# Fewer blocks by seven products, a swiglu gate by Silu, and the last pair of blocks in the down projection's stream

## The chip, the core and the metric

The kernel runs on one core of a Trainium2 chip. The core has five engines with queues of their own: TensorE (PE: matmuls and transposes; its weight loads are listed apart as PEld), VectorE (DVE), ScalarE (ACT), GpSimd (POOL) and SyncE (SP, which here only issues DMAs). Each works through its instructions in order; a semaphore lets one wait for another. The metric is the device time of one execution, in microseconds (us); lower is better.

## The reference

Input x is 256 frames of 2048 features in fp32. Two layers follow each other, each a token mixer (gated linear attention in the first, sparse attention in the second) and a swiglu; a last norm ends it. The part that matters here is the swiglu, which each layer has once:

```python
def swiglu(h, w1, w3, w2):
    return (jax.nn.silu(h @ w1) * (h @ w3)) @ w2

x = x + swiglu(rmsnorm(x, norm_ffn[i]), ffn_w1[i], ffn_w3[i], ffn_w2[i])
```

w1 and w3 are 2048 x 5632, w2 is 5632 x 2048, all fp32. silu(z) is z times the sigmoid of z, which is also z/2 (1 + tanh(z/2)).

## The kernel before

**Numbers in halves.** TensorE takes fp32r operands. To keep fp32's precision every operand is split into a high part (a rounded copy, by ScalarE) and a low part (the rest, by VectorE), and every product is three matmuls: high x high, high x low, low x high. `split_w` (L131 to 137) does this for a weight tile of 512 rows by 512 columns, 128 x 2048 in SBUF: one cast on ScalarE into `wh` (L135), one subtraction on VectorE into `wl` (L136). `wh` and `wl` have three buffers each. A raw weight tile is 1 MB; four buffers (`raw`) hold such tiles. All these loads are issued on SP's queue. `gemm` does the same by L191 and L192.

**The swiglu, `ffn` (L499 to 539).** The 5632 hidden features are cut into 11 blocks (b = 0 to 10) of 512. For a block, x (256 frames in two halves, t = 0 and 1; 2048 features in two halves of eight 128-row slices) is multiplied by 512 columns of w1 and of w3. There are two ways:

- `plain` (L449 to 474): eight products of 128 frames by 1024 features by 512 columns, two of them summed for each of four outputs. That is 8 weight tiles, 8 splits and 192 matmuls of 128 x 128 x 512 (L463). The operands of x are kept as forms: A11, A12, N22 and F7 (a difference of the two halves of frames); the second frame half is got as the first product minus or plus a correction.
- `pair` (L368 to 447): the four blocks of w1 and w3 are taken together with the four of x, as a 2 x 2 matrix product by seven products instead of eight. The operands of x are sums and differences made once per layer (forms A11, A12, N22, F3, F5, F6, F7); the operands of the weights are sums of raw tiles. Some sums are made by VectorE (`plus`, L405), some by a DMA from memory that adds into the tile (`plus_dma`, L408), which goes by GpSimd's queue. It takes 168 matmuls (L393), 8 plain loads, 4 accumulating loads of 1 MB, 14 splits and 4 sums of 128 x 2048 on VectorE. The products come in the order A11, F5, F3, F6, F7, A12, N22. The first operand pair `va` is changed in place by the accumulating loads (after F5 by w3's second half, after F6 by w1's second half), and N22 reads it last. Four tiles hold `va` and `vb`: v0 and v1, and v2 and g3; which pair holds which alternates with `turn`, b // 2 % 2 (L412 to 414). With turn 0, `va` is in v0 and v1.

Both give their results to `done` (L508 to 515): for the first of a frame half, the gate: a Tanh on ScalarE (L512) and a VectorE operation (L513); for the second, a product with it (L515). The result `u` is transposed by TensorE and split (`split_t`, L208 to 219) into one of three operand tiles `g0` to `g2`. `split_t` is a generator in the list `side`, and the matmul loops run one step of it every few matmuls (`tick`).

**The down projection, `pieces` (L476 to 497).** For two blocks that are finished, w2's 1024 rows are multiplied in eight pieces (four output column groups, two blocks), each one weight tile and 24 matmuls (L489 to 491), and the sum is added to x. `ffn` keeps these generators in `down` and runs one piece at each `yield` of the block under way; a pair has eight yields.

**Which way a block takes** is decided by `if down` (L517). After blocks 1, 3, 5 and 7 a down projection is put into `down` (L533). Its eight pieces run in blocks 2, 4, 6 and 8. The generator has then given its eight pieces but has not ended, so that it still stands in `down` when the next block begins, and is dropped at that block's first yield. So blocks 2 to 9 are pairs, the even ones with eight pieces beside them and the odd ones with none; 0, 1 and 10 are plain. The three blocks 8, 9 and 10 are left over, and `residual` multiplies them by w2 after the layer, group by group of output columns, three weight tiles and 72 matmuls for each of four groups. `residual` also adds to x and starts the next norm of each group (`update`, L263; transposes on TensorE, a scaled copy on ScalarE, its low part on VectorE). After the last layer it ends with the final norm (`gemm_tail`, `final`, `last`).

**The order.** The instructions of an engine stand in an order that a scheduler makes from the program; it may move splits, loads and transposes ahead.

Of the kernel before, what the change touches and what calls it, by code (L numbers as in the profile page):

```python
# [12 lines left out]
F32 = mybir.dt.float32  # L13
F32R = mybir.dt.float32r
BF16 = mybir.dt.bfloat16
AF = mybir.ActivationFunctionType
ALU = mybir.AluOpType
AX = mybir.AxisListType

P = 128  # L20
SEQ = 256
NT = SEQ // P
DM = 2048
NB = 512
# [31 lines left out]
def trunk(  # L56
# [7 lines left out]
    nc = tc.nc  # L64
    PS = bass.MemoryType.PSUM
    cst = ctx.enter_context(tc.tile_pool(name="cst", bufs=1))
# [3 lines left out]
    sm = ctx.enter_context(tc.tile_pool(name="sm", bufs=2))  # L70
# [13 lines left out]
            nc.sync.dma_start(x[t][n], x2[t, :, n * NB:(n + 1) * NB])  # L84


    neghalf = cst.tile([P, 8], F32, name="neghalf")
    nc.gpsimd.memset(neghalf, -0.5)
    warm = sm.tile([P, 8], F32, tag="warm", bufs=1, name="warm")
# [4 lines left out]
    cols = cst.tile([P, 72], F32, name="cols")  # L94


    sm.tile([P, 8], F32, tag="pad", bufs=1, name="pad")

    def gains(c0, srcs):

# [30 lines left out]
    def split_w(raw, pool=wp):  # L131

        wh = pool.tile([P, 4, NB], F32R, tag="wh", bufs=3 if pool is wp else 1, name="wh")
        wl = pool.tile([P, 4, NB], F32R, tag="wl", bufs=3 if pool is wp else 1, name="wl")
        nc.scalar.copy(wh, raw)  # L135
        nc.vector.tensor_sub(wl, raw, wh.bitcast(F32))  # L136
        return wh, wl
# [204 lines left out]
    def scaled(r, f, tag, w=NT):  # L342
        o = sm.tile([P, w], F32, tag=tag, name=tag)
        nc.gpsimd.tensor_scalar_mul(o, r, f)
        return o
# [17 lines left out]
    def flush():  # L363
        while side:
            tick()


    def pair(nrm, wa, wb, c0, turn, done):  # L368

        def src(w, j, c):
            r = j * 1024 + c * 512
            return w[r:r + 512, c0:c0 + NB].rearrange("(k p) n -> p k n", p=P)

        def load(w, j, homes):
            o = []
            for c, (pool, tag, bufs) in enumerate(homes):
                raw = pool.tile([P, 4, NB], F32, tag=tag, bufs=bufs, name=tag)
                nc.sync.dma_start(raw, src(w, j, c))  # L380
                o.append(raw)
            return o

        def product(acc, raws, form, start, stop, then=None):
            for c in range(2):
                wh, wl = split_w(raws[c])
                if then is not None:
                    then(c)
                hi, lo = nrm.forms[form]
                for j in range(4):  # L390
                    k = 4 * c + j
                    for i, (l_, r_) in enumerate(((hi, wh), (hi, wl), (lo, wh))):
                        nc.tensor.matmul(acc, l_[:, k, :], r_[:, j, :], start=start and k == i == 0,  # L393
                                         stop=stop and k == 7 and i == 2, skip_group_check=not start)
                    if j % 2:
                        tick()

        def bank():
            return acc_p.tile([P, NB], F32, tag="acc", name="acc")

        def sums(tag):
            return nrm.pool.tile([P, NB], F32, tag=tag, bufs=1, name=tag)

        def plus(dst, other):
            return lambda c: nc.vector.tensor_add(dst[c], dst[c], other[c])  # L405

        def plus_dma(dst, w, j):
            return lambda c: nc.gpsimd.dma_start(dst[c], src(w, j, c), accum_op=ALU.add)  # L408

        fz = nrm.pool  # L410
        stream = [(wp, "raw", RAW)] * 2
        homes = [((fz, "v0", 1), (fz, "v1", 1)), ((fz, "v2", 1), (res, "g3", 1))]  # L412
        va = load(wa, 0, homes[turn])
        vb = load(wb, 0, homes[1 - turn])
        b1 = bank()
        product(b1, va, "A11", True, True, plus(va, vb))
        s1 = sums("s1")
        nc.scalar.copy(s1, b1)
        yield
        b2 = bank()  # L420
        product(b2, va, "F5", True, True, plus_dma(va, wb, 1))
        y = sums("y")
        nc.vector.tensor_sub(y, b2, s1)
        yield
        vc = load(wb, 1, stream)
        product(b2, vc, "F3", False, True, plus(vb, vc))
        yield
        b3 = bank()
        product(b3, va, "F6", True, True, plus_dma(va, wa, 1))
        w = sums("w")  # L430
        nc.vector.tensor_sub(w, b3, s1)
        yield
        product(b3, vb, "F7", False, True)
        nc.vector.tensor_add(w, w, b2)
        nc.vector.tensor_add(y, y, b3)
        yield
        vd = load(wa, 1, stream)
        product(b1, vd, "A12", False, True)
        done("11", b1)
        done("12", w)  # L440
        yield
        product(b3, va, "N22", False, True)
        nc.vector.tensor_sub(s1, s1, b3)
        done("21", s1)
        done("22", y)
        yield
        yield

    def plain(nrm, ws, c0, done):  # L449

        for q, w in zip("12", ws):
            acc = [acc_p.tile([P, NB], F32, tag="acc", name="acc") for _ in range(3)]
            for g in range(4):
                raw = wp.tile([P, 4, NB], F32, tag="raw", bufs=RAW, name="raw")
                nc.sync.dma_start(raw, w[g * NB:(g + 1) * NB, c0:c0 + NB].rearrange("(k p) n -> p k n", p=P))
                wh, wl = split_w(raw)
                for bank, form, start, stop in ((0, "A11", True, True), (1, "F7", True, True)) if g < 2 else \
                        ((0, "A12", False, True), (2, "N22", True, True)):
                    hi, lo = nrm.forms[form]
                    for j in range(4):  # L460
                        k = 4 * (g % 2) + j
                        for i, (l_, r_) in enumerate(((hi, wh), (hi, wl), (lo, wh))):
                            nc.tensor.matmul(acc[bank], l_[:, k, :], r_[:, j, :], start=start and k == i == 0,  # L463
                                             stop=stop and k == 7 and i == 2, skip_group_check=not start)
                        if j % 2:
                            tick()
                if g == 1:
                    s1 = nrm.pool.tile([P, NB], F32, tag="s1", bufs=1, name="s1")
                    nc.scalar.copy(s1, acc[0])
                    nc.vector.tensor_add(s1, s1, acc[1])  # L470
                    yield
            nc.vector.tensor_sub(s1, s1, acc[2])
            done("1" + q, acc[0])
            done("2" + q, s1)
# [24 lines left out]
    def ffn(layer, nrm):  # L499

        w1, w3, w2 = ffn_w1[layer], ffn_w3[layer], ffn_w2[layer]
        sc = {}
        parts = []
        down = deque()
        for b in range(DFF // NB):
            us = [None] * NT

            def done(q, v):  # L508
                t = int(q[0]) - 1
                if q[1] == "1":  # L510
                    us[t] = cm.tile([P, NB], F32, tag="u", name="u")
                    nc.scalar.activation(us[t], v, AF.Tanh, scale=sc["h"][:, t:t + 1])  # L512
                    nc.vector.scalar_tensor_tensor(us[t], us[t], 1.0, v, op0=ALU.add, op1=ALU.mult)  # L513
                else:
                    nc.vector.scalar_tensor_tensor(us[t], us[t], sc["r2"][:, t:t + 1], v, op0=ALU.mult, op1=ALU.mult)  # L515

            for slot, _ in enumerate(pair(nrm, w1, w3, b * NB, b // 2 % 2, done) if down else plain(nrm, (w1, w3), b * NB, done)):  # L517
                if b == 0 and slot == 0:
                    flush()
                    r = nrm.rstd()  # L520
                    sc["h"] = scaled(r, 0.5, "rh")
                    sc["r2"] = sm.tile([P, NT], F32, tag="r2", name="r2")
                    nc.gpsimd.tensor_tensor(sc["r2"], r, sc["h"], op=ALU.mult)
                while down:
                    try:
                        next(down[0])
                        break
                    except StopIteration:
                        down.popleft()
            hi, lo = hi_lo(b % 3)  # L530
            side.append(split_t(us, hi, lo))
            parts.append((hi, lo, b * NB))
            if b % 2 and b < 8:  # L533
                down.append(pieces(w2, parts))
                parts = []
        while down:
            for _ in down.popleft():
                pass
        return w2, parts
# [480 lines left out]
    with tc.tile_pool(name="gp", bufs=2) as gp:  # L1020
        n0.begin(gp)
        down = gla(n0, gp)
        flush()
    with tc.tile_pool(name="fz0", bufs=1) as fz:
        n1.begin(fz)
        residual(gla_w_out[0], down, n1.update)
        down = ffn(0, n1)
        flush()
    with tc.tile_pool(name="dp", bufs=2) as dp:
# [3 lines left out]
        down = dsa(n2, dp)  # L1033
        flush()
    with tc.tile_pool(name="fz1", bufs=1) as fz:
        n3.begin(fz)
        residual(dsa_w_out[0], down, n3.update)
        down = ffn(1, n3)
# [57 lines left out]
```

## Time and profile before

| | us |
|---|---|
| median of 3 runs | 2426.34 (2423.76 to 2428.74) |
| the profiled execution | 2430.86 |
| its span, first to last instruction | 2429.1 |
| TensorE busy | 2281.5 (94%) |
| VectorE busy | 1645.9 (68%) |
| ScalarE busy | 1183.5 (49%) |
| GpSimd busy | 112.8 (5%) |

In the profile, a group's row has the source line, the engine, the operation, its output and inputs with their sizes, how often it ran, then busy time and the mean time of one in ns, then the idle time of the engine just before it and what ended it. A row of a timeline has start and duration in us, and in brackets how long the engine had idled and for what. A row of a stage (start:end) has its length, then busy time and count of instructions for PE, PEld, DVE, ACT and POOL, the granted clock of TensorE as a share, the busy share of the DMA engines, and GB/s. "SPq" is a DMA issue on SP's queue.

The queues of DMAs moved 493 MB in this execution; GpSimd's accumulating loads are 64 of 1 MB.

### The profile page before, as it was taken

How to read it: one execution, taken by the hardware profiler on the slowest of the kernel's cores; microseconds unless marked ns; L12 is line 12 of the kernel's file. 1: busy time of each engine (PE TensorE's matmuls, PEld its weight loads, DVE VectorE, ACT ScalarE, POOL GpSimd, SP SyncE). 2: the span in 40 equal slices, each digit the busy share in tenths (PEclk: the TensorE clock that was granted, in tenths of full speed). 3: DMA queues.
4: the chain of work that ended last, by engine and by line, in shares of the span. 5: the costliest groups of instructions: out<-in, count | busy, mean ns of one | idle time of the engine just before them, and what ended most of it. 6: DMA issues, size and time to landing. Idle time of an engine off the chain costs nothing.

```text
span 2429.1 us, 25156 instructions
## 1 busy us (share of the span) xinstructions
PE 2281.5 (94%) x10199; PEld 1857.5 (76%) x10199; DVE 1645.9 (68%) x1348; ACT 1183.5 (49%) x1053; POOL 112.8 (5%) x159
## 2 busy tenths in 40 slices
PE   9999999998897979989999999999988979889798
PEld 7888888876675867768888888888876867768687
DVE  6555456677886878865556655565786778878754
ACT  5545455454454445544444454454444545545443
POOL 0000000000000000000100000000000000000000
PEclk9999999999999989999999999999998999989899
DMA  8555466586877968775554545566677977779663
GB/s 280 164 174 180 148 219 232 172 233 194 232 242 207 286 184 222 229 205 187 182 173 139 191 157 174 174 219 212 176 235 201 293 182 225 230 190 311 138 218 112
DMA packets 254773, 493.36 MB, mean 203 GB/s; under 512 B 8200, under 2 KB 20832, under 8 KB 254528
## 3 DMA queue, kind: packets, MB, share of 16 engines
q1 hardware_dynamic: 219856, 423.33, 51.1%
q0 software_dynamic: 33792, 67.11, 16.0%
q8 instruction: 80, 1.31, 0.2%
q10 hardware_dynamic: 1008, 1.31, 0.2%
q14 instruction: 37, 0.30, 0.0%
HBM read 489.59 MB, written 2.12 MB: 202 GB/s over the span
## 4 chain that ended last, share of the span: by engine, by line
PE 59%; issue 21%; DMA 9%; DVE 8%; ACT 2%; POOL 1%; SPq 0%; POOLq 0%; ACTq 0%; DVEq 0%
PE acc L201 11%; PE acc L203 11%; PE acc L202 11%; PE acc L463 10%; DMA g<-in_ffn_w 6%; PE acc L393 6%; DVE wl L136 5%; DMA v<-in_ffn_w 3%; PE down L490 2%; ACT wh L135 2%; PE down L491 2%; PE down L489 2%; DVE v L405 1%; POOL v L408 1%; PE trq L827 0%
## 5 line engine op out<-in xcount | busy, mean ns | idle before, releaser
L192 DVE TENSOR_TENSOR wl<-raw,wh 128x2048 fp32r<-128x2048 f32 (+3 forms) x161 | 350.1, 2176 | 314.8 <-ACT wh L191 314.6
L136 DVE TENSOR_TENSOR wl<-raw,wh 128x2048 fp32r<-128x2048 f32 x179 | 409.5, 2289 | 184.7 <-ACT wh L135 184.7
L135 ACT CAST wh<-raw 128x2048 fp32r<-128x2048 f32 x179 | 342.3, 1912 | 392.6 <-PE down L491 144.3
L191 ACT CAST wh<-raw 128x2048 fp32r<-128x2048 f32 (+3 forms) x161 | 291.9, 1815 | 278.8 <-PE acc L203 217.7
L136 DVE TENSOR_TENSOR wl<-v,wh 128x2048 fp32r<-128x2048 f32 x120 | 272.7, 2286 | 83.1 <-ACT wh L135 83.1
L201 PE MATMUL acc<-wh,hh 128*128 128x512 f32 (+3 forms) x832 | 327.1, 393 | 0.0
L135 ACT CAST wh<-v 128x2048 fp32r<-128x2048 f32 x120 | 227.4, 1904 | 198.9 <-DMA v<-in_ffn_w 99.9
L203 PE MATMUL acc<-wh,hl 128*128 128x512 f32 (+3 forms) x832 | 318.4, 383 | 0.0
L202 PE MATMUL acc<-wl,hh 128*128 128x512 f32 (+3 forms) x832 | 317.0, 381 | 0.5 <-DVE wl L192 0.5
L393 PE MATMUL acc<-wh,fhF 128*128 128x512 f32 x512 | 216.5, 426 | 59.3 <-ACT wh L135 59.2
L393 PE MATMUL acc<-wl,fhF 128*128 128x512 f32 x512 | 216.0, 422 | 30.9 <-DVE wl L136 30.9
L490 PE MATMUL down<-wl,g 128*128 128x512 f32 x512 | 204.0, 398 | 9.3 <-DVE wl L136 9.3
L393 PE MATMUL acc<-wh,flF 128*128 128x512 f32 x512 | 212.2, 414 | 0.0
L491 PE MATMUL down<-wh,g 128*128 128x512 f32 x512 | 202.9, 396 | 0.0
L489 PE MATMUL down<-wh,g 128*128 128x512 f32 x512 | 200.3, 394 | 0.0
L203 PEld LDWEIGHTS acc<-wh,hl 128*128 128x128 f32 x832 | 156.2, 188 | 30.8
L202 PEld LDWEIGHTS acc<-wl,hh 128*128 128x128 f32 x832 | 156.6, 188 | 30.3 <-issue 1.7
L201 PEld LDWEIGHTS acc<-wh,hh 128*128 128x128 f32 x832 | 156.5, 188 | 28.9 <-issue 1.9
L393 PEld LDWEIGHTS acc<-wh,fhF 128*128 128x128 f32 x512 | 103.9, 205 | 91.2 <-ACT wh L135 68.3
L201 PE MATMUL acc<-wh,g 128*128 128x512 f32 x424 | 167.2, 394 | 0.0
L203 PE MATMUL acc<-wh,g 128*128 128x512 f32 x424 | 165.5, 390 | 0.0
L202 PE MATMUL acc<-wl,g 128*128 128x512 f32 x424 | 165.4, 390 | 0.0
(282 smaller groups left out, 3608.6 us busy)
## 6 DMA issues: line engine op xcount, KB each, us to landing
raw<-in_ffn_w SPq DMA_DIRECT2D x200, 1024.0 KB, 5.8
v<-in_ffn_w SPq DMA_DIRECT2D x48, 1024.0 KB, 6.6
v<-in_ffn_w POOLq DMA_DIRECT2D x48, 1024.0 KB, 9.4
raw<-in_dsa_w_in SPq DMA_DIRECT2D x48, 1024.0 KB, 5.1
raw<-in_gla_w_in SPq DMA_DIRECT2D x40, 1024.0 KB, 5.1
raw<-in_gla_w_out SPq DMA_DIRECT2D x16, 1024.0 KB, 5.2
g<-in_ffn_w SPq DMA_DIRECT2D x16, 1024.0 KB, 6.7
g<-in_ffn_w POOLq DMA_DIRECT2D x16, 1024.0 KB, 13.3
```

Source lines behind the costliest of these rows:

```text
L135: nc.scalar.copy(wh, raw)
L136: nc.vector.tensor_sub(wl, raw, wh.bitcast(F32))
L191: a = nc.scalar.copy(wh[:, sl, :n], raw[:, sl, :n])
L192: v = nc.vector.tensor_sub(wl[:, sl, :n], raw[:, sl, :n], wh[:, sl, :n].bitcast(F32))
L201: nc.tensor.matmul(acc[t][:, :n], hi[:, k, ts_], wh[:, k, :n], start=start, stop=False)
L202: nc.tensor.matmul(acc[t][:, :n], hi[:, k, ts_], wl[:, k, :n], start=False, stop=False)
L203: nc.tensor.matmul(acc[t][:, :n], lo[:, k, ts_], wh[:, k, :n], start=False, stop=last)
L393: nc.tensor.matmul(acc, l_[:, k, :], r_[:, j, :], start=start and k == i == 0, stop=stop and k == 7 and i == 2, skip_group_check=not start)
L463: nc.tensor.matmul(acc[bank], l_[:, k, :], r_[:, j, :], start=start and k == i == 0, stop=stop and k == 7 and i == 2, skip_group_check=not ...
L489: nc.tensor.matmul(acc[t], hi[:, k, ts_], wh[:, k, :], start=start, stop=False)
L490: nc.tensor.matmul(acc[t], hi[:, k, ts_], wl[:, k, :], start=False, stop=False)
L491: nc.tensor.matmul(acc[t], lo[:, k, ts_], wh[:, k, :], start=False, stop=last)
```

## The change

There are three parts.

1. A block is a pair only if b is 2, 4, 6, 8 or 10; the others (0, 1, 3, 5, 7, 9) are plain. And a down projection is put into `down` after every odd block, so also after 9. It runs in block 10. `residual` is left with one part, block 10, for each layer: 24 matmuls for each of four groups in place of 72.
2. The gate: `Silu` on ScalarE with the norm's factor r as its scale, in place of `Tanh` with r/2 and VectorE's (tanh + 1) times z. The second VectorE operation multiplies with r. Two small GpSimd operations per layer go. Silu is in another activation table than Exp and Tanh: the built program has three more table loads, one ahead of the first Silu of each layer and one ahead of the first Exp of the sparse attention.
3. Two unused tiles. One of 64 bytes at the start of the first pool, and one enlarged by 64 bytes where two tiles of 32 bytes (`r2`) are gone. All the tiles that are used thereby lie 64 bytes further, and keep their distances.

```diff
+    cst.tile([P, 16], F32, name="pad")
...
-    sm.tile([P, 8], F32, tag="pad", bufs=1, name="pad")
+    sm.tile([P, 24], F32, tag="pad", bufs=1, name="pad")
...
-                    nc.scalar.activation(us[t], v, AF.Tanh, scale=sc["h"][:, t:t + 1])
-                    nc.vector.scalar_tensor_tensor(us[t], us[t], 1.0, v, op0=ALU.add, op1=ALU.mult)
+                    nc.scalar.activation(us[t], v, AF.Silu, scale=sc["r"][:, t:t + 1])
                 else:
-                    nc.vector.scalar_tensor_tensor(us[t], us[t], sc["r2"][:, t:t + 1], v, op0=ALU.mult, op1=ALU.mult)
-
-            for slot, _ in enumerate(pair(nrm, w1, w3, b * NB, b // 2 % 2, done) if down else plain(nrm, (w1, w3), b * NB, done)):
+                    nc.vector.scalar_tensor_tensor(us[t], us[t], sc["r"][:, t:t + 1], v, op0=ALU.mult, op1=ALU.mult)
+
+            for slot, _ in enumerate(pair(nrm, w1, w3, b * NB, b // 2 % 2, done) if b in range(2, 11, 2) else plain(nrm, (w1, w3), b * NB, done)):
                 if b == 0 and slot == 0:
                     flush()
                     r = nrm.rstd()
-                    sc["h"] = scaled(r, 0.5, "rh")
-                    sc["r2"] = sm.tile([P, NT], F32, tag="r2", name="r2")
-                    nc.gpsimd.tensor_tensor(sc["r2"], r, sc["h"], op=ALU.mult)
+                    sc["r"] = r
...
-            if b % 2 and b < 8:
+            if b % 2:
                 down.append(pieces(w2, parts))
                 parts = []
```

The order moves with it. On SP's queue, where block 2 of layer 0 ends and block 3 begins, before (L482 loads the down projection's weights, L380 a pair's; the v and g tiles named are block 3's vb and va, then block 4's va):

```order
L380 DMA v_4058<-in_ffn_w 128x4x512
L380 DMA v_4060<-in_ffn_w 128x4x512
L482 DMA raw<-in_ffn_w 128x4x512 x2
L380 DMA raw<-in_ffn_w 128x4x512 x2
L380 DMA v_4054<-in_ffn_w 128x4x512
L380 DMA g_4056<-in_ffn_w 128x4x512
L380 DMA raw<-in_ffn_w 128x4x512 x2
L482 DMA raw<-in_ffn_w 128x4x512 x2
L380 DMA v_4337<-in_ffn_w 128x4x512
L380 DMA v_4339<-in_ffn_w 128x4x512
```

The same place of the changed kernel (L483 and L381 are these lines now, L456 loads a plain block's weights; v_4320 and v_4322 are block 4's va, v_4324 and g_4326 its vb):

```order
L381 DMA v_4320<-in_ffn_w 128x4x512
L381 DMA v_4322<-in_ffn_w 128x4x512
L483 DMA raw<-in_ffn_w 128x4x512 x2
L456 DMA raw<-in_ffn_w 128x4x512 x2
L381 DMA v_4324<-in_ffn_w 128x4x512
L381 DMA g_4326<-in_ffn_w 128x4x512
L456 DMA raw<-in_ffn_w 128x4x512 x6
L483 DMA raw<-in_ffn_w 128x4x512 x2
```

All of block 4's operands are now asked for while block 2 ends, between the second and the third of block 3's eight weight tiles.

On ScalarE, at the end of layer 0's swiglu, before (L469 and L470 of the kernel before belong to block 10, L191 casts the weights of the residual stage, `g` is block 10's operand, L240 is the next norm):

```order
L469 COPY s_7013<-acc 128x512
L191 CAST wh<-raw 128x2048 x3
L787 DMA kvb<-in_dsa_kv_norm 128x256
L217 CAST g_7079<-tr 128x512 x2
L789 DMA kib<-in_dsa_kidx_norm 128x128
L191 CAST wh<-raw 128x2048 x3
L240 ACTIVATE junk,ssq<-x_81 128x512
```

The same place of the changed kernel (L192 casts the residual stage's weights, L513 is the gate):

```order
L192 CAST wh<-raw 128x2048
L513 ACTIVATE u<-s_6813,rstd 128x512
L785 DMA kvb<-in_dsa_kv_norm 128x256
L192 CAST wh<-raw 128x2048
L787 DMA kib<-in_dsa_kidx_norm 128x128
L192 CAST wh<-raw 128x2048
L218 CAST g_7292<-tr 128x512 x2
L192 CAST wh<-raw 128x2048
```

Three casts of residual weights stand ahead of the two copies of block 10's operand in both; in the changed kernel the first residual matmul needs these copies, where before it needed those of block 8. With three buffers for `wh`, the third of the casts takes the one that the last piece's matmuls read.

On VectorE, the same place of the changed kernel (L193 makes the low parts of the residual weights, L497 adds the last piece to x, L219 makes the low parts of block 10's operand, L356 adds the first residual group to x):

```order
L444 TENSOR_TENSOR s_6813<-s_6813,acc 128x512
L193 TENSOR_TENSOR wl<-raw,wh 128x2048
L515 SCALAR_TENSOR_TENSOR u<-u,rstd,y 128x512
L193 TENSOR_TENSOR wl<-raw,wh 128x2048
L497 TENSOR_TENSOR x_87<-x_87,down_7228 128x512
L497 TENSOR_TENSOR x_88<-x_88,down_7229 128x512
L193 TENSOR_TENSOR wl<-raw,wh 128x2048
L219 TENSOR_TENSOR g_7292<-tr,g_7292 128x512 x2
L356 TENSOR_TENSOR x_81<-x_81,acc_7319 128x512
```

The low part of the third residual weight stands ahead of block 10's low parts. On TensorE the eight transposes of block 10 stand directly behind the last piece and ahead of the first residual matmul, and the sequence of blocks 4, 6, 8 and 10 is that of block 2, matmul for matmul.

## The prediction

> **What bounds the kernel now.** I read the page first (TensorE is busy for 94% of the span, so time is lost only where it waits), then busy time by stage over both feed-forward layers. The stages are cut at the first matmul of each block, which the timeline of TensorE shows by its line and tiles. In order: blocks 0 and 1 together; blocks 2, 3, 4, 5 and 6; blocks 2 to 9 together; block 10; the residual stage.
>
> ```profile
> PE 2281.5 (94%) x10199; PEld 1857.5 (76%) x10199; DVE 1645.9 (68%) x1348; ACT 1183.5 (49%) x1053; POOL 112.8 (5%) x159
> ```
>
> ```profile
> core 0: us, PE busy (x) PEld busy (x) DVE busy (x) ACT busy (x) POOL busy (x), PEclk, DMA share, GB/s
> 395.86:485.92 90.06, 90.03 (x402) 73.62 (x400) 56.78 (x46) 42.00 (x39) 1.87 (x3) 1.00 0.64 210
> 485.92:571.08 85.16, 83.33 (x370) 68.23 (x369) 69.50 (x46) 44.62 (x27) 5.41 (x4) 1.00 0.85 247
> 571.08:630.64 59.56, 44.48 (x177) 34.10 (x176) 40.28 (x26) 28.29 (x18) 5.17 (x4) 0.91 0.77 200
> 630.64:718.20 87.56, 84.01 (x369) 68.22 (x368) 76.45 (x50) 45.53 (x28) 5.19 (x4) 1.00 0.83 248
> 718.20:777.60 59.40, 44.69 (x177) 34.15 (x176) 40.28 (x26) 28.30 (x18) 5.19 (x4) 0.91 0.77 200
> 777.60:866.09 88.49, 84.34 (x370) 68.12 (x368) 76.39 (x50) 45.33 (x28) 5.19 (x4) 1.00 0.83 246
> 485.92:1072.00 586.08, 516.59 (x2178) 411.91 (x2177) 461.56 (x294) 294.41 (x183) 41.71 (x32) 0.96 0.80 222
> 1072.00:1117.24 45.24, 45.24 (x206) 37.11 (x204) 27.29 (x21) 19.63 (x16) 0.00 (x0) 1.00 0.61 210
> 1117.24:1186.05 68.81, 68.81 (x320) 56.68 (x318) 38.47 (x35) 31.54 (x38) 0.68 (x4) 1.00 0.54 174
> ```
>
> Blocks 0, 1 and 10 (plain) and the residual stage keep TensorE full. Block 2 (a pair beside a down projection) is nearly full. Blocks 3, 5, 7 and 9 are pairs with nothing beside them: some 59 us for 168 matmuls, with TensorE busy for 45. The chain of waits gives the full pace, 24 matmuls in 5.49 us, so 0.2288 us each:
>
> ```profile
> 669.19 5.49 PE acc L393 x24
> ```
>
> 168 such matmuls are 38.4 us. What holds an odd block is the chain of its four accumulating loads on GpSimd's queue, each issued when the one before has landed (first and last of four), behind which ScalarE's split and then the last product wait:
>
> ```profile
> 580.42 1.28 POOL L408 DMA_DIRECT2D v<-in_ffn_w  x1 [49.62 <-issue]
> ...
> 609.99 1.30 POOL L408 DMA_DIRECT2D g<-in_ffn_w  x1 [7.63 <-DVE wl L136]
> 623.71 1.91 ACT L135 CAST wh<-g 128x2048 fp32r<-128x2048 f32 x1 [4.64 <-DMA g<-in_ffn_w]
> ```
>
> From 580.4 to 623.7 is 43 us for four loads. In an even block the down projection's 192 matmuls cover the same chain.
>
> **The change, part by part.** Sums are against the profiled execution: span 2429.1 us, 2430.86 in all, 4.5 us above the median of the runs, 2426.34.
>
> *Odd blocks, pair to plain.* Each goes from 168 matmuls to 192, loses its accumulating loads, and becomes what blocks 0 and 1 are: 90.06/2 = 45.03 us with their transposes. Four cost 180.1 us.
>
> *Even blocks.* Block 2 is now the model of all five (4, 6, 8 now follow a plain block as it does; 10 becomes one), in the same order on TensorE. Its 85.16 us hold one wait of 2.25 us: the second half of the F6 product needs the second accumulating load.
>
> ```profile
> 520.44 1.91 ACT L135 CAST wh<-g 128x2048 fp32r<-128x2048 f32 x1 [6.88 <-DMA g<-in_ffn_w]
> ```
>
> In blocks whose accumulating loads go to v0 and v1 (4 and 8) the F6 product ran at full pace (the row at 669.19 is block 4's). So I take 85.16 for 2, 6, 10 and 85.16 - 2.25 = 82.9 for 4 and 8: 421.3 us in layer 0. Bounds: no such wait anywhere (-6.8), and 2.25 us in all five (+4.5).
>
> In layer 1 the rows are, in order, block 2, blocks 2 to 9, block 10, the residual stage, and what follows the last matmul:
>
> ```profile
> 1718.69:1802.95 84.26, 83.10 (x369) 68.14 (x368) 69.39 (x46) 44.63 (x27) 5.23 (x4) 1.00 0.85 249
> 1718.69:2309.38 590.69, 527.15 (x2177) 421.85 (x2176) 461.86 (x294) 294.86 (x183) 41.53 (x32) 0.93 0.79 221
> 2309.38:2354.60 45.22, 45.22 (x205) 37.11 (x204) 27.46 (x21) 19.62 (x16) 0.00 (x0) 1.00 0.61 210
> 2354.60:2421.00 66.40, 66.24 (x295) 54.30 (x293) 35.32 (x32) 26.15 (x28) 0.56 (x1) 1.00 0.42 142
> 2421.00:2429.10 8.10, 0.00 (x0) 0.00 (x0) 2.03 (x5) 2.06 (x4) 0.55 (x1) 0.79 0.35 130
> ```
>
> Its five even blocks: 3 x 84.26 + 2 x 82.9 = 418.6. Up to the residual stage, then: layer 0 goes from 586.08 + 45.24 = 631.3 to 421.3 + 180.1 = 601.4 (**-29.9**), layer 1 from 590.69 + 45.22 = 635.9 to 598.7 (**-37.2**).
>
> *Residual stage, three parts to one.* 288 matmuls become 96, 22.0 us. It now starts with block 10's own operand, which nothing covers. In the order of ScalarE and VectorE given above, the split of a third residual weight stands ahead of the copies of that operand, and this split needs the buffer that the last down matmuls read. The same wait stands behind block 2:
>
> ```profile
> 571.32 1.91 ACT L135 CAST wh<-v 128x2048 fp32r<-128x2048 f32 x1 [3.52 <-PE down L491]
> 573.13 0.58 ACT L217 CAST g<-tr 128x512 fp32r<-128x512 f32 x1
> ...
> 573.74 0.69 DVE L218 TENSOR_TENSOR g<-tr,g 128x512 fp32r<-128x512 f32 x1
> ```
>
> ```profile
> L136 DVE TENSOR_TENSOR wl<-raw,wh 128x2048 fp32r<-128x2048 f32 x179 | 409.5, 2289 | 184.7 <-ACT wh L135 184.7
> ```
>
> From the last down matmul (571.08): 0.24 to the split, 1.91, its low part on VectorE 2.29, the operand's low part 0.69, with 0.1 between: 5.2 us, in which TensorE does eight transposes and two matmuls. Entry costs 5.2 - 0.4 = 4.8 us beyond the 96 matmuls, twice; bounds 0.8 (eight transposes alone, at the 0.1 us each that comes next) and 7.1 (one more split on VectorE in front). Layer 0 keeps the transposes of the next norm: 68.81 - 288 x 0.2288 = 2.9 us for 28, so 2.5 for 24. Layer 0: 4.8 + 22.0 + 2.5 = 29.3 against 68.81 (**-39.5**). What could spill is VectorE's work per output group: the low parts of the norm's operand cost
>
> ```profile
> L256 DVE SCALAR_TENSOR_TENSOR hl<-tr,cols,hh 128x256 fp32r<-128x256 f32 x32 | 13.7, 477 | 5.5 <-ACT hh L253 5.5
> ```
>
> each, and four of them, two x updates of 0.69 and one split of 2.29 are 5.6 us beside TensorE's 5.5 + 0.6. I take no spill; with one it is about a microsecond in each of four groups.
>
> Layer 1: 4.8 + 22.0 = 26.8 to the last matmul and 8.2 behind it, against 66.40 + 8.10. The final tile of the first half used to finish 8.2 us ahead of the second; now it is 12 matmuls, 2.75 us. VectorE needs 3.7 us from one x update to the end of its last scaling:
>
> ```profile
> 2412.62 0.69 DVE L1057 TENSOR_TENSOR x<-x,acc 128x512 f32<-128x512 f32 x1 [5.96 <-PE acc L154]
> ...
> 2415.59 0.75 DVE L1064 SCALAR_TENSOR_TENSOR x<-x,rf,nf 128x512 f32<-128x512 f32 x1
> ```
>
> So the second half starts 1.0 us late: 26.8 + 8.2 + 1.0 = 36.0 against 74.5 (**-38.5**).
>
> *Silu for Tanh.* 44 VectorE operations on 128x512 go (30 us at the 0.69 of such an operation above), and 44 activations change function:
>
> ```profile
> L512 ACT ACTIVATE u<-s,rh 128x512 f32<-128x512 f32 x22 | 15.9, 722 | 8.6 <-DVE s L443 8.6
> L604 ACT ACT_TABLE_LOAD x2 | 2.6, 1283 | 0.0
> ```
>
> The trace shows no Silu. Nearest row 0.72 us; bounds 0.58 (the copy at 573.13) and 1.44 (twice the row); I take 0.72. What hides it: the gate is due two pieces (10.9 us) or half a block later. Uncovered, 44 x 0.7 = 31 us at worst. The 30 us shorten nothing, as TensorE doesn't wait for VectorE in plain blocks (45.24 of 45.24 us busy in block 10). Three more table loads of 1.283 us fall where ScalarE idles 2 to 3 us at a time: nothing, at most 3.8. The Trainium skill ("ScalarE: Activation LUTs", "What ACT_TABLE_LOAD costs") puts a switch at 2.66 us with its drain; uncovered, the sum would be higher by an estimated 8 us.
>
> *Pads.* All tiles move by the same 64 bytes, so operands keep their rests to each other. Two groups of one operation whose operands differ in just that, by 64 of 128 bytes, are row L136 above and this one:
>
> ```profile
> L136 DVE TENSOR_TENSOR wl<-v,wh 128x2048 fp32r<-128x2048 f32 x120 | 272.7, 2286 | 83.1 <-ACT wh L135 83.1
> ```
>
> 3 ns apart; over some 500 splits 1.5 us of VectorE either way, and I take nothing.
>
> *Sum:* -29.9 - 39.5 - 37.2 - 38.5 = -145.1; 2430.86 - 145.1 = 2285.8 for a run like the profiled one, 4.5 less, **2281 us**, at the median's level.
>
> The clock column shows 1.00 where TensorE is full and 0.91 in odd blocks, so a part of their 59 us is half-rate time after the waits, and goes with them. The Trainium skill ("TensorE: Matmul & The Clock Gate", "Part 1: The HAM clock gate") has the clock halve after an idle window of about 3.4 us; odd blocks agree. By that rule the two residual entries might each bring one such window, an estimated 1.7 us each, and 2284; this trace cannot say, since transposes and two matmuls break the idle time there.
>
> **Rivals.** *A, the even blocks keep their lateness.* Blocks 4 and 6 took 87.56 and 88.49, which is 4.7 and 3.3 over what I give them, by waits at their start. If a steady state and not the odd pair makes these, eight blocks pay: 4 x 4.7 + 4 x 3.3 = 32, so 2313 us. For it: every even block but 2 shows them. Against it: block 4's operands were asked for late, at 607.32 and up to 627.97, since block 3 held their tiles (SP's own queue):
>
> ```profile
> 554.56 0.37 SPq L380 DMA_DIRECT2D g<-in_ffn_w  x1
> ...
> 583.86 5.37 SPq L482 DMA_DIRECT2D raw<-in_ffn_w  x2
> 607.32 2.57 SPq L380 DMA_DIRECT2D v<-in_ffn_w  x2
> ...
> 627.97 0.37 SPq L380 DMA_DIRECT2D g<-in_ffn_w  x1
> ```
>
> A plain block holds none of these tiles. *B, slower.* The change adds 2 x 72 matmuls net, 32.9 us; it loses if plain blocks wait too. SP's queue is in order, and in the new order the next pair's v and g loads stand ahead of a plain block's last six weight loads; while they wait for the old pair's last product, nothing behind them is issued. It needs 145/8 = 18 us of wait in each odd block, which is the length of the queue's own pause before 607.32 (from 583.86 + 5.37). Then about 2430 or more. Against it: block 2 released those tiles by 554.56, 16 us before block 3 began, and block 3's third weight is due 11 us after that. *C, cheaper:* no F6 waits and covered entries, -11 and -8, so about 2262.
>
> **How the numbers follow.** Forecast 0.80, A 0.10 (2301 to 2325), C 0.05 (2255 to 2267), B 0.03, and 0.02 for a gain that is mostly eaten. The range is the forecast's own, 2267 to 2301: 2281 - 11 (no F6 waits) - 3 (part of the entries) below; above, the bounds' +4.5 and +4.6, +4 for VectorE in the residual stage, +3.8 for table loads and +3 for half-rate windows. The others hold two in ten. A measurement tells 0.2% (5 us) from no change: faster 0.96, within it 0.015, slower 0.025.
>
> **What would show it.** In the changed profile: odd blocks of 45 us with TensorE full and clock 1.00; even blocks of 83 to 85 us with no wait ahead of F5; 40 accumulating loads for 64; residual stages of about 29 and 27 us, whose one gap is at the entry, behind VectorE's low part; a tail of 9 us. Wrong are odd blocks above 48, even blocks above 87, or an entry above 8.

## The result, and the profile after

The changed kernel takes **2283.47 us** (median of 4 runs, 2280.6 to 2289.56), the kernel before, run beside it, 2427.06 (2423.76 to 2428.74): a ratio of 0.9413, with a 95% interval of 0.9392 to 0.9435. The profiled execution took 2283.89 us, with a span of 2282.1 (2429.1 before).

The first part of the page has busy time and share of the span of each engine:

```profile
PE 2254.4 (99%) x10343; PEld 1856.3 (81%) x10343; DVE 1499.3 (66%) x1254; ACT 1127.5 (49%) x1026; POOL 79.3 (3%) x131
```

TensorE has 144 matmuls more and is busy 27 us less (2254.4 against 2281.5): what went was stretched time, not work. The stages, cut as in the view of before (length, then busy time and count of PE, PEld, DVE, ACT, POOL, granted clock, DMA share, GB/s), are blocks 2 to 6, block 10, blocks 2 to 10 together and the residual stage of layer 0; then, of layer 1, blocks 2 to 10, the residual stage and what follows the last matmul:

```profile
485.49:570.11 84.62, 83.23 (x369) 68.22 (x368) 66.05 (x43) 44.69 (x27) 5.42 (x4) 1.00 0.88 261
570.11:614.99 44.88, 44.88 (x201) 36.85 (x200) 26.68 (x18) 18.86 (x14) 0.00 (x0) 1.00 0.51 164
614.99:698.65 83.66, 83.28 (x370) 68.24 (x369) 66.06 (x43) 44.77 (x27) 5.17 (x4) 1.00 0.88 264
698.65:743.51 44.86, 44.86 (x202) 36.84 (x200) 26.68 (x18) 18.86 (x14) 0.00 (x0) 1.00 0.51 164
743.51:827.37 83.86, 83.28 (x370) 68.23 (x369) 66.05 (x43) 44.69 (x27) 5.19 (x4) 1.00 0.89 263
1000.28:1087.32 87.04, 85.10 (x369) 69.32 (x368) 66.31 (x43) 44.66 (x27) 5.87 (x8) 0.98 0.74 202
485.49:1087.32 601.83, 597.54 (x2641) 489.63 (x2640) 437.21 (x279) 299.05 (x191) 26.83 (x24) 1.00 0.75 225
1087.32:1115.54 28.22, 26.26 (x130) 21.22 (x129) 19.50 (x26) 16.09 (x29) 0.00 (x0) 1.00 0.48 157
1647.60:2247.36 599.76, 595.49 (x2641) 488.50 (x2640) 437.37 (x279) 300.79 (x192) 25.98 (x20) 1.00 0.75 226
2247.36:2273.05 25.69, 23.55 (x105) 18.64 (x103) 15.29 (x22) 8.16 (x18) 0.56 (x1) 1.00 0.00 1
2273.05:2282.10 9.05, 0.01 (x1) 0.00 (x0) 3.00 (x7) 3.20 (x6) 0.55 (x1) 0.62 0.60 232
```

The odd blocks (44.88, 44.86) have no idle time left and a clock of 1.00. The even ones still hold a wait, and it stands in every one of them: what is over 82.9 us, the length without it (shown below, in the run with the waits covered). In block 10 it is 4.1 us. The timeline of that place shows GpSimd's accumulating loads, ScalarE's split that needs the second of them, and TensorE in the middle of the F6 product, where the second half of the weights begins:

```profile
1010.94 1.29 POOL L409 DMA_DIRECT2D v<-in_ffn_w  x1 [95.75 <-issue]
1019.94 1.30 POOL L409 DMA_DIRECT2D g<-in_ffn_w  x1 [7.71 <-DMA v<-in_ffn_w]
1035.33 1.29 POOL L409 DMA_DIRECT2D v<-in_ffn_w  x1 [14.09 <-DMA g<-in_ffn_w]
```

```profile
1035.12 1.92 ACT L136 CAST wh<-g 128x2048 fp32r<-128x2048 f32 x1 [7.13 <-DMA g<-in_ffn_w]
```

```profile
1037.09 0.50 PE L394 MATMUL acc<-wh,fhF 128*128 128x512 f32 x1
1039.41 0.71 PE L394 MATMUL acc<-wl,fhF 128*128 128x512 f32 x1 [1.82 <-DVE wl L137]
1039.92 0.63 PE L394 MATMUL acc<-wh,flF 128*128 128x512 f32 x1
1040.35 0.63 PE L394 MATMUL acc<-wh,fhF 128*128 128x512 f32 x1
```

Each load is issued when the one before has landed, 9 and then 15 us later. The second is split at 1035.12, and VectorE's low part follows 2.3 us behind. TensorE loses not only the idle 1.82 us: the matmuls behind it start 0.43 us apart in place of 0.2288, until 1042.9.

### The profile page after: what moved, and what is told of

It is laid out like the page before. It is cut to its first block, busy times and chain, and to the rows that moved or that the text cites. A ratio compares the mean times of both kernels' runs of the same rounds, so it can differ in the third digit from the quotient of the medians.

```text
span 2282.1 us, 25208 instructions
## 1 busy us (share of the span) xinstructions
PE 2254.4 (99%) x10343; PEld 1856.3 (81%) x10343; DVE 1499.3 (66%) x1254; ACT 1127.5 (49%) x1026; POOL 79.3 (3%) x131
## 4 chain that ended last, share of the span: by engine, by line
PE 68%; issue 20%; DMA 5%; DVE 4%; ACT 2%; POOL 0%; POOLq 0%; ACTq 0%; SPq 0%
PE acc L464 14%; PE acc L204 11%; PE acc L202 11%; PE acc L203 11%; PE acc L394 8%; PE down L490 3%; PE down L491 3%; DMA g<-in_ffn_w 3%; PE down L492 3%; DVE wl L137 2%; DMA v<-in_ffn_w 2%; ACT wh L136 1%; DVE v L406 1%; PE tr L216 1%; PE trq L825 0%
## 5 line engine op out<-in xcount | busy, mean ns | idle before, releaser
L137 DVE TENSOR_TENSOR wl<-raw,wh 128x2048 fp32r<-128x2048 f32 x217 | 496.8, 2290 | 261.3 <-ACT wh L136 261.3
L193 DVE TENSOR_TENSOR wl<-raw,wh 128x2048 fp32r<-128x2048 f32 (+3 forms) x147 | 317.8, 2164 | 276.4 <-ACT wh L192 276.3
L192 ACT CAST wh<-raw 128x2048 fp32r<-128x2048 f32 (+3 forms) x147 | 265.5, 1809 | 230.8 <-PE acc L204 194.6
L492 PE MATMUL down<-wh,g 128*128 128x512 f32 x640 | 249.0, 389 | 0.0
L490 PE MATMUL down<-wh,g 128*128 128x512 f32 x640 | 247.5, 389 | 0.0
L137 DVE TENSOR_TENSOR wl<-v,wh 128x2048 fp32r<-128x2048 f32 x72 | 164.3, 2287 | 44.6 <-ACT wh L136 44.6
L136 ACT CAST wh<-v 128x2048 fp32r<-128x2048 f32 x72 | 137.4, 1908 | 97.0 <-PE acc L394 39.2
L464 PE MATMUL acc<-wh,fhA 128*128 128x512 f32 x384 | 152.2, 396 | 0.1
L464 PE MATMUL acc<-wh,flA 128*128 128x512 f32 x384 | 150.4, 392 | 0.0
L464 PE MATMUL acc<-wl,fhA 128*128 128x512 f32 x384 | 149.8, 390 | 0.0
L490 PEld LDWEIGHTS down<-wh,g 128*128 128x128 f32 x640 | 120.1, 188 | 25.5
L491 PEld LDWEIGHTS down<-wl,g 128*128 128x128 f32 x640 | 120.1, 188 | 25.3
L492 PEld LDWEIGHTS down<-wh,g 128*128 128x128 f32 x640 | 120.1, 188 | 25.0
L394 PE MATMUL acc<-wl,fhF 128*128 128x512 f32 x320 | 127.8, 399 | 8.4 <-DVE wl L137 8.4
```

Source lines behind the costliest of these rows:

```text
L192: a = nc.scalar.copy(wh[:, sl, :n], raw[:, sl, :n])
L193: v = nc.vector.tensor_sub(wl[:, sl, :n], raw[:, sl, :n], wh[:, sl, :n].bitcast(F32))
L490: nc.tensor.matmul(acc[t], hi[:, k, ts_], wh[:, k, :], start=start, stop=False)
L491: nc.tensor.matmul(acc[t], hi[:, k, ts_], wl[:, k, :], start=False, stop=False)
L492: nc.tensor.matmul(acc[t], lo[:, k, ts_], wh[:, k, :], start=False, stop=last)
```

## The experiments

### Which part of the change brings the gain

**Odd blocks alone.** The kernel before with blocks 3, 5, 7 and 9 plain, and nothing else changed:

```diff
-... if down else plain(...)
+... if b in range(2, 9, 2) else plain(...)
```

> The kernel before, in which blocks 3, 5, 7 and 9 are plain; Tanh, the pads, block 10 plain and a residual of three blocks stay. Theory (the odd pairs' accumulating loads are the loss): blocks 2 to 9 take 4 x 84 + 4 x 44.8 = 515 us in place of 586 in layer 0 and 591 in layer 1, so 2427 - 147 = 2280 us, the whole gain of the change; a residual stage of 69 us as before, and block 10 of 45. What the prediction booked as two terms of the residual stage (-39.5 and -38.5) would then be only work moved into block 10, which brings nothing by itself. Rival (the two parts each bring what the prediction's terms say): the odd blocks bring 4 x 14.4 + 3.3 + 4.7 + 4 = 70 us at most per layer without block 10, but block 10's pair and the short residual bring further time: about 2300 or more here.

Measured: 2286.06 us (2285.14 to 2286.76), ratio 0.9418 (0.94 to 0.9436). Blocks 2 to 9 of both layers:

```profile
485.86:1002.01 516.15, 512.33 (x2274) 420.33 (x2272) 376.90 (x251) 253.75 (x164) 20.96 (x16) 1.00 0.73 222
1648.67:2165.09 516.42, 512.38 (x2274) 420.34 (x2273) 376.88 (x251) 253.90 (x164) 20.78 (x16) 1.00 0.73 222
```

They took 586.08 and 590.69 before: -69.9 and -74.3, together -144.2 us of the 147.0 by which the span of the whole change is shorter. By the medians this run is 2.6 us above the changed kernel's 2283.47, and the two intervals overlap. So this is the whole gain, as far as the runs can tell, and the rival's 2300 is out. The expectation's 2280 took the savings, counted in the profiled execution of 2430.86, off the median of 2427.

**The last pair alone.** The kernel before, whose odd blocks stay pairs, with block 10 as a pair beside blocks 8 and 9's down projection:

```diff
-... if down else plain(...)
+... if b >= 2 else plain(...)
...
-if b % 2 and b < 8:
+if b % 2:
```

> The kernel before, in which blocks 2 to 9 stay pairs, block 10 is a pair too, and a down projection for blocks 8 and 9 runs in it; the residual has one block. Theory (this part only moves work: 45.2 us of block 10 and 68.8 and 74.5 of the residual stage with its tail become a pair block of 85 to 88 and 29 and 36): layer 0 114.0 to 114.5 to 117, layer 1 119.7 to 120.5 to 124; so 2427 + 1 to + 8, 2428 to 2435 us. Rival (moving the pieces beside a pair covers waits and saves time): 2410 us or less.

Measured: 2441.19 us (2435.66 to 2444.49), ratio 1.0056 (1.0039 to 1.0073), some 14 us slower. Block 10:

```profile
1075.57:1164.80 89.23, 85.63 (x370) 69.32 (x369) 74.51 (x49) 45.53 (x28) 5.87 (x8) 0.98 0.73 207
```

Behind an odd pair it is late, as blocks 4 and 6 were in the kernel before (87.56 and 88.49). So the part saves nothing by itself, and costs where the pairs stand close. It cost more than expected; in the profile 5.3 and 4.0 us of the 10 lie from block 9 to the end of the residual stage, and the rest is spread over the other blocks. In the changed kernel it comes out even: block 10 and what follows it take 87.04 + 28.22 in layer 0 against 45.24 + 68.81, and 84.0 + 25.69 + 9.05 against 45.22 + 66.40 + 8.10 in layer 1: +1.2 and -0.9.

**What held the odd pairs.** The kernel before; GpSimd's four loads in an odd pair overwrite the tile in place of adding to it, so those sums are missing:

```diff
+            if not adds:
+                return lambda c: nc.gpsimd.dma_start(dst[c], src(w, j, c))
             return lambda c: nc.gpsimd.dma_start(dst[c], src(w, j, c), accum_op=ALU.add)
...
-... pair(nrm, w1, w3, b * NB, b // 2 % 2, done) if down ...
+... pair(nrm, w1, w3, b * NB, b // 2 % 2, done, b % 2 == 0) if down ...
```

> The kernel before, in which GpSimd's four loads of each odd pair block overwrite their tile in place of adding to it: those sums are left out, everything else of the pair stays (tiles, bytes from memory, products, order, the waits on these loads). Theory (an odd block is as long as its chain of four accumulating loads, each 8.4 to 15 us from issue to landing): a load without addition lands sooner, and blocks 3, 5, 7 and 9 take 42 to 50 us in place of 59, the whole 2427 - 8 x 9 to 8 x 17 = 2290 to 2355 us. Rival (what holds an odd block is that its tiles come free late, or the bytes of its loads): 55 to 60 us each, over 2390 us.

Measured: 2341.2 us (two runs), ratio 0.9637 (0.9608 to 0.9666). Blocks 3 and 5:

```profile
569.76:620.08 50.32, 43.68 (x177) 34.48 (x176) 41.55 (x27) 28.74 (x18) 3.07 (x4) 0.93 0.71 246
706.40:756.07 49.67, 43.40 (x178) 34.41 (x176) 41.39 (x27) 28.73 (x18) 3.06 (x4) 0.93 0.70 247
```

59.5 us became 50, at the upper edge of what was expected, with the same bytes from memory, the same tiles and the same products. So loads that add were the last wait, for 9.5 of the 14.6 us by which an odd pair was longer than a plain block. Two things went with the addition, and the run does not separate them. A load of block 3 lands after 5.6 to 8.0 us in place of 8.6 to 13.6. And the second load is issued 1.6 us after the first, where before it followed 9.8 us later, when the first had landed:

```profile
579.10 0.79 POOL L409 DMA_DIRECT2D v<-in_ffn_w  x1 [49.55 <-issue]
580.73 0.77 POOL L409 DMA_DIRECT2D g<-in_ffn_w  x1 [0.85 <-DVE wl L136]
```

TensorE's first two waits in block 3 are now behind VectorE's low part, and behind a split that itself waits for VectorE's sum:

```profile
578.17 0.50 PE L393 MATMUL acc<-wl,fhF 128*128 128x512 f32 x1 [1.61 <-DVE wl L136]
586.76 0.74 PE L393 MATMUL acc<-wh,fhF 128*128 128x512 f32 x2 [3.05 <-ACT wh L135]
```

```profile
584.81 1.90 ACT L135 CAST wh<-v 128x2048 fp32r<-128x2048 f32 x1 [1.85 <-DVE v L405]
```

Without the addition VectorE is the likely next bound of a pair alone: 14 splits and 4 sums of 2.29 us are 41 us, for 38.4 us of matmuls.

### The gate and the unused spaces

**Tanh in the changed kernel.** The gate of before and its two `r2` tiles are back (the lines that make r/2 and `r2` are left out here), and neither space is added, so that every distance is the same again. That is the kernel before with the first part of the change alone:

```diff
-nc.scalar.activation(us[t], v, AF.Silu, scale=sc["r"][:, t:t + 1])
+nc.scalar.activation(us[t], v, AF.Tanh, scale=sc["h"][:, t:t + 1])
+nc.vector.scalar_tensor_tensor(us[t], us[t], 1.0, v, op0=ALU.add, op1=ALU.mult)
...
```

> The changed kernel with the gate of before: Tanh on ScalarE, then two VectorE operations, and the smaller second pad. Theory (the gate lies beside TensorE's work in either form): within 0.2% of the changed kernel, 2279 to 2288 us; VectorE busy 30 us more. Rival (VectorE's time counts, since F6 and the residual's entry wait behind it): 4 to 15 us more, 2288 to 2298. Second rival (Silu's table loads or its duration cost): 2275 or less.

Measured: 2282.36 us (2281.54 to 2285.47), ratio 0.9406 (0.939 to 0.9423): the same as with Silu. So the first part of the change brings the whole gain, and the gate with the spaces nothing that can be told. VectorE is busy 1525.7 us in place of 1499.3, beside TensorE's work. In the groups of the changed kernel Silu lasts 724 ns, where Tanh took 722. Nor do the three more table loads of 1283 ns show in the time:

```profile
L513 ACT ACTIVATE u<-s,rstd 128x512 f32<-128x512 f32 x22 | 15.9, 724 | 2.1 <-DVE s L444 2.1
L513 ACT ACT_TABLE_LOAD x2 | 2.6, 1283 | 1.8 <-PE acc L464 1.8
L979 ACT ACT_TABLE_LOAD x1 | 1.3, 1283 | 0.0
```

**Without the two unused spaces:**

```diff
-    cst.tile([P, 16], F32, name="pad")
...
-    sm.tile([P, 24], F32, tag="pad", bufs=1, name="pad")
+    sm.tile([P, 8], F32, tag="pad", bufs=1, name="pad")
```

> The changed kernel without its two unused spaces of 64 bytes: the pools that come behind the one with the small tiles then lie 64 bytes nearer to those ahead of it, so that raw weight tiles and v tiles have the same rest by 128 bytes where they were 64 apart. Theory (the rests of operands cost 3 ns of 2287 in VectorE's subtraction): within 0.2% of the changed kernel, 2279 to 2288 us, and the mean of VectorE's low parts between 2280 and 2295 ns. Rival (the rests decide an operation's speed): the means of casts, subtractions or sums change by over 2%, and the time by over 5 us.

Measured: 2296.44 us (2296.02 to 2298.73), ratio 0.9464 (0.9448 to 0.948): 13 us slower than the changed kernel, so the theory falls; but not by the rival's engine either. The subtractions take 2291 and 2288 ns, the casts 1912: nothing there moved. What moved is the pace of TensorE. The chain of waits lists products of 24 matmuls (first row), and a plain block shows the same (second row):

```profile
633.25 5.59 PE acc L393 x24
```

```profile
575.70:621.20 45.50, 45.50 (x202) 36.96 (x200) 26.86 (x18) 18.82 (x14) 0.00 (x0) 1.00 0.48 162
```

5.59 in place of 5.49, and 45.50 in place of 44.88, at a clock of 1.00. Pieces of the down projection keep 5.44 to 5.46 in both kernels. The products read x's forms and the weight tiles, which the missing spaces bring to another distance (384 bytes beyond a multiple of 1024 in place of 448); the pieces read `g` and the weight tiles, whose distance stays. Two more runs of the changed kernel varied that distance:

```diff
-    sm.tile([P, 24], F32, tag="pad", bufs=1, name="pad")
+    sm.tile([P, 40], F32, tag="pad", bufs=1, name="pad")
```

> The changed kernel with its second unused space 64 bytes larger, so that the forms of x (TensorE's stationary operands in the products) lie 512 bytes beyond a multiple of 1024 from the weight tiles (its moving operands), where they lie 448 in the changed kernel and 384 in the run without the spaces. Measured so far: 24 matmuls of a product take 5.59 us at 384, 5.49 at 448, and 5.44 in a piece, whose operand lies at 0. Theory (a matmul's pace goes by the distance of its two operands within some power of two up to 512 bytes): 5.44 us per 24, 8 us less over 3984 matmuls of the products, some 5 less in the other stages: 2268 to 2278 us. Rival (the distance 64 from a multiple of 128 is what makes 448 better than 384): 5.59 us as without the spaces, about 2297.

```diff
-    cst.tile([P, 16], F32, name="pad")
...
-    sm.tile([P, 24], F32, tag="pad", bufs=1, name="pad")
+    sm.tile([P, 168], F32, tag="pad", bufs=1, name="pad")
```

> The changed kernel with the first unused space gone and the second 576 bytes larger, so that forms and weight tiles lie a multiple of 1024 bytes apart, as the pieces' operand and the weight tiles do. Theory (the distance of a matmul's two operands sets its pace): 24 matmuls of a product take 5.44 us as those of a piece: 2268 to 2278 us. Rival (products are at another pace than pieces for another reason, their order or their bank of sums): 5.49 or more, 2280 or more.

Measured: 2286.2 us (2285.28 to 2291.5), ratio 0.9415 (0.9396 to 0.9434), with a distance of 512, and 2277.36 (2272.51 to 2281.58), ratio 0.9371 (0.9352 to 0.9391), with a multiple of 1024. The pace is as the theory has it in both: a plain block takes 44.46 us, here of the first:

```profile
568.79:613.25 44.46, 44.46 (x201) 36.83 (x200) 26.57 (x18) 18.86 (x14) 0.00 (x0) 1.00 0.52 166
```

But the time followed only in part: by the medians the second is 6 us below the changed kernel, at the upper edge of the 2268 to 2278 expected of both, and the first, 3 us above it, misses them. In the profile of the first, the F6 products took 9.8 us in layer 0 and 15.1 in layer 1 beyond their matmuls' pace (7.6 and 5.6 in the changed kernel). The reading is that the loads keep their own pace, so that a faster TensorE meets them sooner; the runs with the waits covered, below, test it. The time of both runs also scatters over 6 and 9 us, as the changed kernel's does (9 us); waits for loads that land after 12.8 to 15.3 us could make it so.

What sets the pace can be narrowed down. The weight tiles lie at the same addresses in the kernel before, in the run without the spaces and in the one with a multiple of 1024, where 24 matmuls take 5.49, 5.59 and 5.44 us; so it is not the weights' own place. From the kernel before to the changed one both operands move by 64 bytes at one distance, and the pace stays at 5.49. That speaks for the distance; that the forms' own place has a part in it is not wholly ruled out.

### The waits covered

In each even block a piece of the down projection is moved from behind A12 to between F3 and F6, and block 10's transposes are queued ahead of its last piece:

```diff
         product(b2, vc, "F3", False, True, plus(vb, vc))
         yield
+        yield
...
         done("12", w)
-        yield
         product(b3, va, "N22", False, True)
...
+                if b == 10 and slot == 7:
+                    hi, lo = hi_lo(b % 3)
+                    side.append(split_t(us, hi, lo))
...
-            hi, lo = hi_lo(b % 3)
-            side.append(split_t(us, hi, lo))
+            if b < 10:
+                hi, lo = hi_lo(b % 3)
+                side.append(split_t(us, hi, lo))
```

> The changed kernel with two waits covered: in each even block a second piece of the down projection stands between F3 and F6 (it stood behind A12), and the transposes of block 10's operand are queued ahead of the last piece in place of behind it. Theory: the F6 waits (7.6 + 5.6 us in the profile of the changed kernel) vanish since the first half of F6 starts 5.5 us later, and about 2 of the 2.7 us go at each residual entry: 2283.5 - 13.2 - 4 = 2266 us, 2262 to 2271. Rival (each wait comes back later, at A12 or N22, where the later accumulating loads are due, or at the piece that is now missing behind A12): 2276 to 2284.

Measured: 2266.78 us (2266.31 to 2268.08), ratio 0.9331 (0.9314 to 0.9348), as the theory has it. Block 2 and block 3:

```profile
485.58:568.49 82.91, 82.91 (x369) 68.31 (x368) 66.33 (x43) 44.85 (x27) 5.42 (x4) 1.00 0.89 266
568.49:613.35 44.86, 44.86 (x201) 36.85 (x200) 26.68 (x18) 18.84 (x14) 0.00 (x0) 1.00 0.51 164
```

No F6 product waits in either layer, and the first residual matmul follows the last transposes without a wait. The runs scatter over 1.8 us.

With that cover, the distance was tried again (multiple of 1024, then 512):

> The changed kernel with the two waits covered and the distance of forms and weight tiles a multiple of 1024 bytes. Covered waits alone gave 2266.8 us with 5.49 us for 24 matmuls of a product; the distance alone gave 5.44 but its time went up and down with the F6 waits (20.4 us in its profile against 13.2). Theory (the faster products ran into the accumulating loads, which go at their own pace; with the piece moved that cover holds): 3984 matmuls of products at 2.1 ns less are 8.4 us, the other stages some 4: 2266.8 - 12 = 2254 us, 2251 to 2258. Rival (the gain is eaten by another wait): 2262 to 2268.

> The same with a distance that is a multiple of 512 but not of 1024 bytes. With this distance alone the matmuls were as fast (5.44 us for 24) but the kernel took 2286 us, no less than the changed kernel's 2283.5, with 24.4 us of F6 waits. Theory (only those waits ate the gain): as with a multiple of 1024, 2254 us, 2251 to 2258. Rival (this distance costs elsewhere, on ScalarE, VectorE or in the loads): 2262 or more.

Measured: 2257.44 us (2256.05 to 2258.33), ratio 0.9295 (0.9278 to 0.9312), and 2256.11 (2255.75 to 2257.87), ratio 0.9291 (0.9274 to 0.9309). Both distances now give the same within 2 us, 9 to 11 us less than the cover alone, as expected. Of the second, block 2 and a product:

```profile
484.37:567.03 82.66, 82.66 (x370) 68.19 (x368) 66.27 (x43) 44.95 (x27) 5.42 (x4) 1.00 0.89 267
```

```profile
623.58 5.44 PE acc L394 x24
```

So the waits had eaten the gain of the faster products, a part of it at the one distance and all of it at the other. The last one, 2256 us, beats both kernels: 27 us below the changed one.

## Why the prediction was right, point by point

| | forecast | measured |
|---|---|---|
| an odd block | 45.03 | 44.88, 44.86 |
| layer 0, block 2 to the residual stage | 601.4 | 601.83 |
| layer 1, the same | 598.7 | 599.76 |
| residual stage, layer 0 | 29.3 | 28.22 |
| residual stage and tail, layer 1 | 36.0 | 25.69 + 9.05 = 34.74 |
| all | -145.1 | -147.0 of the span |

- **What bounds the odd pairs** was read rightly: without the addition they fell to 50 us. The text took the four loads as the whole of it; the run shows their addition as 9.5 of 14.6 us, with waits for VectorE's results behind it.
- **Odd and even blocks.** Block 2 was the right model. Rival A is out: blocks 4, 6 and 8 do not start late, so the lateness came from the odd pairs. So is B: no plain block waits. C, no F6 waits and covered entries, did not come about by itself either; where both were covered, the kernel took 2267 us, against the 2262 that C was priced at.
- **The F6 waits** were mis-sized in their parts. The prediction tied them to the tiles that take the accumulating loads, none in blocks 4 and 8 and 2.25 in the others. They stand in all five, at 0.3 to 4.1 us; the sum of layer 0 came out near (7.6 against 6.75), by luck. Why the second load lands after 13 us in one block and 15 in another is not settled.
- **The residual entry** was 4.8 us in the forecast and is 28.22 - 22.0 - 2.5 = 3.7. The chain was right, but TensorE does eight matmuls with the operand's high part while the low part is made, not two:

```profile
1087.33 1.04 PE L216 MATMUL tr<-ident,u 128*128 128x128 f32 x8
1089.97 0.50 PE L202 MATMUL acc<-wh,g 128*128 128x512 f32 x1 [1.60 <-ACT g L218]
...
1092.42 0.73 PE L204 MATMUL acc<-wh,g 128*128 128x512 f32 x2 [0.35 <-DVE g L219]
```

- **The clock.** By the rule of the Trainium skill ("TensorE: Matmul & The Clock Gate", "Part 1: The HAM clock gate") each entry might have brought half-rate time, and 2284 us. The idle pieces are 1.60 and 0.35 us, and the matmuls behind them keep their pace: no half-rate time there, so on this point the rule and the trace agree. In block 10 rule and trace differ: half-rate time follows an idle piece of 1.82 us, shorter than the window of about 3.4 us that the prediction took from the rule. There the measurement decides, and the forecast for even blocks had no such term.
- **Where the gain is booked.** The sum was right, its rows mislead. -29.9 and -37.2 stand beside the blocks, -39.5 and -38.5 beside the residual stage, as if each part of the change brought half. But block 10 as a pair pays for what the residual stage saves. By the runs, the odd blocks bring 141 us (2427 to 2286), and the last pair none that can be told.
- **Silu** costs and brings nothing, as forecast.
- **The spaces** cost nothing against the kernel before, as forecast, since they keep the distances. The reason given looked at VectorE alone. What the spaces hold in place is TensorE's pace: with the two small tiles gone and no space in their stead, the kernel takes 13 us more.

## What to carry to other kernels

Where a change moves work from one stage to another, put the two stages in one sum before booking a gain to either. When an engine is full but for short waits, cover the waits before making it faster: with the waits left, faster matmuls brought six microseconds at one distance and none at the other, and nine to eleven at both when nothing was left for them to run into. And where tiles are added, removed or resized, look at the pace of matmuls that have nothing to do with them: their operands may have moved.

## What the runs showed that was not expected

- **Matmuls of one shape have three paces** here, which go with the distance of the stationary and the moving operand in SBUF: 24 matmuls of 128 x 128 x 512 take 5.59 us at 384 bytes beyond a multiple of 1024, 5.49 at 448, 5.44 at 512 and 0. Other distances were not tried, and why it is so stays open. The Trainium skill ("SBUF — State Buffer", "Who interferes with whom") calls TensorE's two read ports independent of each other; a pace that goes with the distance of what they read, by up to 2.8%, does not follow from that, and no run shows whether the ports are the reason.
- **An accumulating load of 1 MB** is 8.3 to 15.4 us from issue to landing in these runs, in even blocks mostly in alternation (9 and 15 us in the rows above), where the same load without the addition took 5.5 to 8.
- **A wait of 1.82 us can cost nearly twice that.** In block 10 the matmuls behind it start 0.43 us apart seven times, some 1.6 us beyond their pace in all. Other waits of the same length, in the run with a distance of 512, were followed by full pace at once:

```profile
1038.99 0.50 PE L394 MATMUL acc<-wl,fhF 128*128 128x512 f32 x1 [1.82 <-DVE wl L137]
1039.33 0.40 PE L394 MATMUL acc<-wh,flF 128*128 128x512 f32 x1
```
